# Mixture-of-experts stage in two multiplication passes of 32 places, with packed 2 MB weight loads and two more load places

## The chip, the core and the metric

One Trainium2 chip, of which this program uses one core. Times are device microseconds (us) of one launch, the median of 3 runs. The core has TensorE (PE) for matrix products, with weight loads (PEld) that overlap the products, VectorE (DVE), ScalarE (ACT), GpSimd (POOL) and SyncE (SP, which here only issues DMAs). Lines such as L323 are lines of the kernel before.

## The reference, cut to what matters

256 tokens of width 1024 go through two blocks in float32. The first has a mixer, a cross-attention and a mixture of experts; the second has feed-forward layers, sparse attention and a gated mixer. The change sits in the mixture of experts:

```python
D_MODEL = 1024; SEQ = 256; N_EXPERTS = 32; TOP_K = 2; D_EXPERT = 512
def hierarchical_moe(xn, w_rg, b_rg, w_re, b_re, w_g, w_u, w_d):
    ...                      # a group of 8 experts, then the best 2 of the group, for each token
    def expert_block(args):
        xb, e = args         # the tokens of one expert
        hb = jax.nn.silu(xb @ w_g[e]) * (xb @ w_u[e])
        return hb @ w_d[e]
    ...
    y = y_pad[dest] * gates[order][:, None]
    out = jnp.zeros((t, d), xt.dtype).at[token_idx[order]].add(y)
x = x + hierarchical_moe(rms_norm(x, norm_ffn[l]), ...)
```

`w_g` and `w_u` are 1024x512 and `w_d` is 512x1024 for each expert: 6.29 MB an expert in float32, 201.3 MB for all 32. 256 tokens by 2 experts make 512 assignments. In the reference's inputs (seed 0) the fullest expert gets 29 of them.

## The kernel before

Every large weight is streamed once. `weight_plan` lists the stages' weights as pieces of 128 partitions by up to 2048 columns (1 MB). `fetch` loads a piece into a `raw` place (R_RAW = 4 places of 1 MB; in the expert stage the two tiles `xh` and `xl` of the pool "moe" serve once as spare places) by a DMA on the SP queue, straight from the weight's own layout, so that a partition's row of a DMA is 512 to 4096 bytes long. `prepare` splits a piece into a high part `wh` (a cast on ACT, L296) and the rest `wl` (a subtraction on DVE, L297), both of type fp32r. Of `wh` and `wl` there are three places each (R_W = 3): `ahead` prepares the piece that lies two beyond the one in use, so a cast waits until PE is done with the piece three before it. A `raw` place is free once the subtraction has read it.

The activations are split in the same way, and `mm3` (L322 to L324) makes each product out of three passes: high by high, high by low, low by high.

In `moe`, the router on DVE computes which two experts each token takes, and its place among that expert's tokens. While that runs, ACT scales the tokens by the norm (L942, into `xs`), casts them to `xsh` (L943), and POOL makes `xsl` (L944), for one half of the tokens after the other. Each expert owns CAP = 42 places, three experts (EPB) fill a block of 128 places, and there are 11 blocks, two to a group. `prep` builds a 0/1 matrix `Sg` for a group, gathers tokens into places by products with it (L1056), with the norm's gain multiplied in when the result is split into `xh` and `xl` (L1060, L1061), and transposes `Sg` into `ST` (L1068, L1070). `expert_up` makes the gate and up products (2 weights x 8 rows x 3 passes = 48 products of 512 columns), the silu (L1229), the masked product `eh` (L1231), four transposes (L1234) and a split (`ehh` L327, `ehl` L328). `down` makes 4 x 2 x 3 = 24 products more, summed over the three experts of a block in PSUM. At a block's end `gathered` scales and splits the result into `yh` and `yl` (L1086, L1087), and `spread` adds it to the tokens by products with `ST` (L1096 to L1098). If an expert had more than 42 tokens, `overflow` would run all 32 experts again over all tokens, behind a branch on the loaded flag `rflag`.

The tile framework's scheduler sets the order of the instructions of each engine; it interleaves the code's pieces, as the rows in the section on the change show. An engine takes its instructions in that order. The stages follow one another as in `STAGES`: mix, cross, moe, fin1, f00, ma, f01, f10, mb, f11, fin2. The last seven are called the second block here.

## Time and profile before

| | us |
|---|---|
| median of 3 runs | 1921.79 (1920.49 to 1922.55) |
| the profiled execution | 1921.77 |
| its span on the core | 1920.0 |
| its expert stage, from the first expert's products to the second block's | 219.5 to 816.5, that is 597.0 |
| routing, between the last product of the cross-attention and the first of the experts | about 198 to 219.5 |

The profile gives, for each engine, how long it was busy and in how many instructions, what an instruction's engine waited for ahead of it, and what the DMAs moved. A product's busy time overlaps the next one's; the pace is the distance between two starts. Where DMA is given a share, it is the mean busy share of the core's 16 DMA engines.

### The profile page before, as it was taken

What the parts mean: (1) busy time and instruction counts of PE and PEld (TensorE: products, weight loads), DVE (VectorE), ACT (ScalarE), POOL (GpSimd) and SP (SyncE); (2) the same over time, 40 slices, a digit from 0 to 9 for tenths busy, and PEclk for the clock granted to TensorE, in tenths of its full rate; (3) what the DMA queues carried; (4) which work ended last, traced back from release to release, by engine and by line L of the source; (5) the groups of instructions that cost most, each with busy time, mean ns of one, the idle gap of its engine ahead of it and who ended that gap; (6) DMA issues with size and microseconds to landing.
All of it is one profiled execution on the core that took longest, in us unless ns stands there. A gap on an engine that the chain in (4) does not pass through costs nothing. (4 is left out here: it accounts for less than half of the span.)

```text
span 1920.0 us, 23872 instructions
## 1 busy us (share of the span) xinstructions
PE 1882.6 (98%) x9268; PEld 1572.8 (82%) x9268; DVE 1357.6 (71%) x1751; ACT 1071.3 (56%) x1318; POOL 30.6 (2%) x43
## 2 busy tenths in 40 slices
PE   8999699999999999999999999999999999999998
PEld 7888588878888888788889988888888888888886
DVE  6986888889888888875549755545554669566554
ACT  5755676777767777654444554444444544455443
POOL 1000100000000000000000000000000000000000
PEclk9999899999999999999999999999999999999999
DMA  8344499999999999966456455556555855666552
GB/s 269 117 169 153 147 335 332 335 330 334 344 329 346 334 342 337 334 208 211 171 181 199 160 163 188 177 175 203 189 178 177 294 178 176 185 199 194 177 185 77
DMA packets 264180, 438.39 MB, mean 228 GB/s; under 512 B 10784, under 2 KB 133936, under 8 KB 263680
## 3 DMA queue, kind: packets, MB, share of 16 engines
q1 hardware_dynamic: 261136, 424.85, 66.0%
q0 software_dynamic: 2496, 11.32, 1.8%
q8 instruction: 74, 1.21, 0.3%
q10 hardware_dynamic: 432, 0.66, 0.1%
q14 instruction: 42, 0.34, 0.1%
HBM read 435.67 MB, written 2.63 MB: 228 GB/s over the span
## 5 line engine op out<-in xcount | busy, mean ns | idle before, releaser
L297 DVE TENSOR_TENSOR wl<-raw,wh 128x2048 fp32r<-128x2048 f32 (+2 forms) x603 | 931.0, 1564 | 406.5 <-ACT wh L296 404.6
L296 ACT CAST wh<-raw 128x2048 fp32r<-128x2048 f32 (+2 forms) x603 | 780.4, 1322 | 498.4 <-PE acc L324 329.9
L322 PE MATMUL acc<-wh,xh 128*128 128x512 f32 x1424 | 561.6, 394 | 0.7 <-PEq L1167 0.7
L323 PE MATMUL acc<-wl,xh 128*128 128x512 f32 x1424 | 559.0, 393 | 3.1 <-DVE wl L297 2.1
L324 PE MATMUL acc<-wh,xl 128*128 128x512 f32 x1424 | 556.6, 391 | 0.0
L323 PEld LDWEIGHTS acc<-wl,xh 128*128 128x128 f32 x1424 | 267.6, 188 | 64.3 <-DVE wl L297 11.4
L322 PEld LDWEIGHTS acc<-wh,xh 128*128 128x128 f32 x1424 | 267.5, 188 | 54.6 <-ACTq L1167 0.8
L324 PEld LDWEIGHTS acc<-wh,xl 128*128 128x128 f32 x1424 | 267.4, 188 | 54.7
L322 PE MATMUL acc<-wh,hhi 128*128 128x512 f32 x352 | 137.6, 391 | 0.0
L324 PE MATMUL acc<-wh,hlo 128*128 128x512 f32 x352 | 137.0, 389 | 0.0
L323 PE MATMUL acc<-wl,hhi 128*128 128x512 f32 x352 | 137.0, 389 | 0.0
L322 PE MATMUL acc<-xh,wh 128*128 128x256 f32 x352 | 102.0, 291 | 2.3 <-ACT wh L290 2.3
L324 PE MATMUL pmi<-wh,ehl 128*128 128x512 f32 x256 | 101.5, 397 | 0.0
L324 PE MATMUL acc<-xh,wl 128*128 128x256 f32 x352 | 101.2, 289 | 0.3 <-DVE wl L291 0.3
L323 PE MATMUL acc<-xl,wh 128*128 128x256 f32 x352 | 101.4, 289 | 0.0
L323 PE MATMUL pmi<-wl,ehh 128*128 128x512 f32 x256 | 100.5, 393 | 0.0
L322 PE MATMUL pmi<-wh,ehh 128*128 128x512 f32 x256 | 94.9, 395 | 0.0
L601 ACT ACTIVATE sg<-acc,rs_o 128x256 f32<-128x256 f32 x66 | 31.3, 475 | 94.1 <-PE acc L324 94.0
L324 PEld LDWEIGHTS acc<-wh,hlo 128*128 128x128 f32 x352 | 66.1, 188 | 13.8
L323 PEld LDWEIGHTS acc<-wl,hhi 128*128 128x128 f32 x352 | 66.1, 188 | 13.6
L322 PEld LDWEIGHTS acc<-wh,hhi 128*128 128x128 f32 x352 | 66.1, 188 | 13.4
L322 PEld LDWEIGHTS acc<-xh,wh 128*128 128x128 f32 x352 | 67.9, 194 | 3.8 <-ACT wh L290 2.7
(409 smaller groups left out, 2043.5 us busy)
## 6 DMA issues: line engine op xcount, KB each, us to landing
raw<-in_ffn_w_in_dram SPq DMA_DIRECT2D x176, 512.0 KB, 4.8
raw<-in_w_e_gate_dram SPq DMA_DIRECT2D x64, 1024.0 KB, 7.0
raw<-in_w_e_down_dram SPq DMA_DIRECT2D x64, 1024.0 KB, 7.0
raw<-in_w_e_up_dram SPq DMA_DIRECT2D x62, 1024.0 KB, 7.1
raw<-in_ffn_w_out_dram SPq DMA_DIRECT2D x40, 1024.0 KB, 5.0
raw<-in_a_w_in_dram SPq DMA_DIRECT2D x14, 1024.0 KB, 5.1
raw<-in_b_w_in_dram SPq DMA_DIRECT2D x12, 1024.0 KB, 5.5
raw<-in_b_w_in_dram SPq DMA_DIRECT2D x16, 768.0 KB, 4.5
```

The source lines that it names most:

```text
L296: self.nc.scalar.copy(h[:, ks], raw[:, ks])
L297: self.nc.vector.tensor_tensor(l[:, ks], raw[:, ks], h[:, ks].bitcast(F32), ALU.subtract)
L322: mm(ps, ah, bh, start=start, stop=False)
L323: mm(ps, ah, bl, start=False, stop=False)
L324: mm(ps, al, bh, start=False, stop=stop)
L601: nc.scalar.activation(sg, ps[:, :256], AF.Silu, scale=rstd[:, t:t + 1])
```

## The change

**Two passes.** CAP is 32, EPB is 2, so a block of 128 places holds for each of two experts 32 places of high parts and beside them 32 of low parts of the same tokens. One operand `xb` so holds both parts, and each weight is multiplied in two passes, by `wh` and by `wl` (L1135, L1136, L1165, L1166 of the kernel after; 48 products of 512 columns an expert in place of 72). The four products high and low by high and low are then all there; high and low places are added by a product with a 0/1 matrix `fold` of 32 columns, which also transposes: 8 products of type float32 an expert (`act`, L1147), for which ACT first copies each PSUM result to `eg0` or `eg1` (L1138). The transposes, the mask and the split of 512 columns go; silu, product and split are now 128 columns wide (L1149 to L1153) and write into `eh0` or `eh1`, whose other half stays zero. There are 16 blocks in 8 groups of 4 experts. A gather writes 128 places for each part (L1093) and is cast by ACT alone (L1095). `y` is no longer split: `spread` multiplies `ST` and `y` in float32 (L1126), one half of tokens and columns at a time, taken from a list `todo`, one an expert.

**The norm's gain** is multiplied in ahead of the gather: POOL loads `norm_ffn` and multiplies the tokens by it into `xs` (L980), for each half of the tokens, with one `xs` for both.

**Loads.** The class `Plan` takes the place of `weight_plan`. The host lays every streamed weight out in the order of use, two pieces side by side, so that one DMA of 2 MB reads 16 KB in a row for each partition. (The first six pieces of the program are loaded one by one.) There are R_RAW = 2 places of 2 MB, free when the second piece has been prepared, and MORE = 2 places more for the loads of the stages cross and moe.

```diff
-R_RAW = 4
+R_RAW = 2
-CAP = 42
-EPB = 3
+CAP = 32
+EPB = 2
+NB = NE // EPB
+GE = 4
+MORE = 2
...
+        key, place, members = self.plan.loads[i]
+        pool = self.free.pop(0)
+        raw = pool.tile([P, 4096], F32, name=self.n("raw"), tag="raw")
+        width, at = sum(self.plan.cols(j) for j in members), 0
+        self.nc.sync.dma_start(raw[:, :width],
+                               self.io["w_" + key][place:place + P * width].rearrange("(p c) -> p c", p=P))
...
+        if self.plan.load_of.get(i + 1) != self.plan.load_of[i]:
+            self.free.append(pool)
...
+            if self.more is not None and self.plan.loads[self.fetched][0] not in ("cross", "moe"):
+                self.free = [pool for pool in self.free if pool is not self.more]
...
+                nc.gpsimd.tensor_tensor(xs, self.x[:, t], gb, ALU.mult)
+                nc.scalar.activation(xs, xs, AF.Copy, scale=rstd[:, t:t + 1])
...
+                    for part, src in enumerate((xsh, xsl)):
+                        for t in range(NT):
+                            nc.tensor.matmul(pt[:, part * P:(part + 1) * P], src[:, t, k * P:(k + 1) * P], Sg[:, t],
+                                             start=t == 0, stop=t == NT - 1)
+                    nc.scalar.copy(xb[:, k].rearrange("p (e a s) -> p e a s", a=2, s=CAP),
+                                   pt.rearrange("p (a e s) -> p e a s", a=2, s=CAP))
...
+                for n, (ST, y) in enumerate(blocks):
+                    nc.tensor.matmul(pu, ST[:, t * P:(t + 1) * P], y[:, hf], start=n == 0, stop=n == len(blocks) - 1)
...
+                        nc.tensor.matmul(ps, xb[:, kk], wh[:, k], start=kk == 0, stop=False)
+                        nc.tensor.matmul(ps, xb[:, kk], wl[:, k], start=False, stop=kk == KD - 1)
+                sb = self.t(pool, [P, 512], "eg" + str(w), 2)
+                nc.scalar.copy(sb, ps)
...
+                for w in range(2):
+                    for k in range(4):
+                        nc.tensor.matmul(ph[:, w, k], gu[w][:, k * P:(k + 1) * P], fold, start=True, stop=True)
+                sg = self.t(pool, [P, 4, CAP], "esg", 2)
+                nc.scalar.activation(sg, ph[:, 0], AF.Silu)
+                nc.vector.tensor_tensor(sg, ph[:, 1], sg, ALU.mult)
+                h, o = hs[e % EPB], (e % EPB) * 2 * CAP
+                nc.scalar.copy(h[:, :, o:o + CAP], sg)
+                nc.vector.tensor_tensor(h[:, :, o + CAP:o + 2 * CAP], sg, h[:, :, o:o + CAP].bitcast(F32), ALU.subtract)
...
+                    nc.tensor.matmul(yb[hf], h[:, kk], wh[:, kk % 2, cs], start=first and kk == 0, stop=False)
+                    nc.tensor.matmul(yb[hf], h[:, kk], wl[:, kk % 2, cs], start=False, stop=end and kk == 3)
```

Three places in the order of the instructions follow; a number behind a name is that of its buffer.

TensorE before, within one expert's down products (`pmi` is their PSUM tile, L322 to L324 the three passes, L1234 the transposes of the next expert):

```order
L324 MATMUL pmi_3145<-wh_3384,ehl_3294 128x512
L323 MATMUL pmi_3146<-wl_3385,ehh_3293 128x512
L324 MATMUL pmi_3146<-wh_3384,ehl_3294 128x512
L1234 MATMUL ptr_3422<-pack_77,eh_3420 128x128 x4
L322 MATMUL pmi_3145<-wh_3384,ehh_3293 128x512
L323 MATMUL pmi_3145<-wl_3385,ehh_3293 128x512
L324 MATMUL pmi_3145<-wh_3384,ehl_3294 128x512
```

After the transposes of the next expert, the passes over `ehh` and `ehl` go on three by three. TensorE after, from the end of one expert's down products into the next gate products (`acc`; L1093 is a gather, L1147 the fold, L1126 the spread):

```order
L1165 MATMUL pmi_3676<-wh_3662,eh_2113 128x512
L1166 MATMUL pmi_3676<-wl_3663,eh_2113 128x512
L1165 MATMUL pmi_3677<-wh_3662,eh_2113 128x512
L1166 MATMUL pmi_3677<-wl_3663,eh_2113 128x512
L1093 MATMUL ptr_3720<-Sg_3574,xsh_2117 128x128 x2
L1093 MATMUL ptr_3720<-Sg_3574,xsl_2118 128x128 x2
L1135 MATMUL acc_3726<-wh_3680,xb_3079 128x512
L1147 MATMUL ptr_3755<-pack_87,eg_3631 128x32 x4
L1147 MATMUL ptr_3755<-pack_87,eg_3674 128x32 x4
L1126 MATMUL ptr_3827<-y_3292,ST_2841 128x512
L1136 MATMUL acc_3726<-wl_3681,xb_3079 128x512
```

The product by `ehl` has gone, and eight folds and a float32 spread stand between two products of a gate.

ScalarE before, over two experts (L296 casts pieces, L1229 is the silu, L327 the split's cast):

```order
L1229 ACTIVATE esg_4001<-acc_3927 128x512
L296 CAST wh_3967<-raw_3884 128x2048
L296 CAST wh_3985<-raw_3928 128x2048
L327 CAST ehh_4010<-ptr_4005 128x512
L296 CAST wh_4020<-raw_3946 128x2048
L296 CAST wh_4038<-raw_3965 128x2048
L1060 ACTIVATE xh_3756<-ptr_4054,pack_77 128x256
```

A silu, then casts with single casts or scalings of other tiles between them. ScalarE after (L332 casts pieces, now two of one `raw` load in a row, L1138 copies a PSUM result, L1149 is the silu, L1152 the cast into `eh`, L1095 the gather's):

```order
L332 CAST wh_3903<-raw_3770 128x2048
L332 CAST wh_3915<-raw_3770 128x2048
L1138 COPY eg_3927<-acc_3900 128x512
L332 CAST wh_3933<-raw_3799 128x2048
L332 CAST wh_3945<-raw_3799 128x2048
L1149 ACTIVATE esg_4013<-ptr_4004 128x128
L332 CAST wh_3978<-raw_3858 128x2048
L332 CAST wh_3990<-raw_3858 128x2048
L1138 COPY eg_4002<-acc_3975 128x512
L1152 CAST eh_2114<-esg_4013 128x4x32
L1095 CAST xb_4091<-ptr_4092 128x256
```

After every second cast there is now a copy, silu or cast that waits for a product of PE.

GpSimd before, during routing:

```order
L927 DMA esel_2141<-in_c_esel_dram 128x352
L929 IOTA iota_2143 128x256
L262 DMA gb_7092<-in_norm_final_dram 128x1024
L944 TENSOR_TENSOR xsl_2151<-xs_2152,xsh_2150 128x1024
L944 TENSOR_TENSOR xsl_2151<-xs_2156,xsh_2150 128x1024
L1166 TENSOR_LOAD rflag_2221
```

The two subtractions follow each other with nothing of POOL's own between them. GpSimd after (L980 is the product with the gain, L983 the subtraction that was L944):

```order
L295 DMA gx_2119<-in_norm_ffn_dram 128x1024
L980 TENSOR_TENSOR gx_2119<-x,gx_2119 128x1024
L963 IOTA iota_2115 128x128
L971 MEMSET eh_2113 128x512
L971 MEMSET eh_2114 128x512
L983 TENSOR_TENSOR xsl_2118<-gx_2119,xsh_2117 128x1024
L980 TENSOR_TENSOR gx_2119<-x,gx_2119 128x1024
L983 TENSOR_TENSOR xsl_2118<-gx_2119,xsh_2117 128x1024
```

The second product with the gain stands between the two subtractions.

## Rows read from the trace of the kernel before

**Rows 1.** Four stretches, cut at the routing and at the ends of the expert stage: busy us of PE, PEld, DVE, ACT and POOL (instructions in brackets), granted TensorE clock, DMA share, GB/s.

```profile
0.00:200.00 200.00, 186.80 (x1158) 161.21 (x1158) 151.04 (x372) 123.22 (x264) 10.69 (x15) 1.00 0.56 181
200.00:219.50 19.50, 9.07 (x49) 8.41 (x49) 16.61 (x63) 7.96 (x16) 4.73 (x2) 0.65 0.21 83
219.50:816.50 597.00, 592.52 (x2739) 483.23 (x2739) 523.46 (x394) 429.09 (x347) 0.00 (x0) 1.00 0.95 330
816.50:1920.00 1103.50, 1094.24 (x5325) 920.00 (x5323) 666.48 (x923) 511.07 (x694) 15.16 (x26) 1.00 0.57 184
```

**Rows 2.** Waits within the expert stage (219.5 to 816.5): who waited for whom, us in total, times, longest.

```profile
DVE wl L297 <- ACT wh L296: 60.6, 95, 1.9
...
ACT wh L296 <- PE acc L324: 22.0, 35, 2.1
ACT wh L296 <- DMA raw<-in_w_e_down_dram: 21.3, 24, 2.2
```

**Rows 3.** PE's instructions in order of time (start us, us) at two places of the expert stage: products of 512 columns and gathers of 256; gathers of 128 columns, and four records of float32 products of 32 columns.

```profile
603.29 0.39 PE L322 MATMUL acc<-wh,xh 128*128 128x512 f32 x1
...
605.33 0.40 PE L322 MATMUL acc<-wh,xh 128*128 128x512 f32 x1
605.57 0.28 PE L1056 MATMUL ptr<-Sg,xsh 128*128 128x256 f32 x1
605.69 0.28 PE L1056 MATMUL ptr<-Sg,xsl 128*128 128x256 f32 x1
...
750.27 0.27 PE L1056 MATMUL ptr<-Sg,xsl 128*128 128x128 f32 x1
...
750.94 0.27 PE L1056 MATMUL ptr<-Sg,xsl 128*128 128x128 f32 x1
...
753.89 0.62 PE L1073 MATMUL ptr<-rG,Sg 128*128 128x32 f32 x4
```

**Rows 4.** Float32 products of 384 columns in the second block, as a group over the whole run (8 channel groups by 2 halves of the tokens are 16 products in the code).

```profile
L1464 PE MATMUL ptr<-vn,wsT 128*128 128x384 f32 x32 | 11.6, 485 | 0.0
```

**Rows 5.** The chain that ended last, at one place of the second block: the time at which PE had the chain, and the us of four records of the group in rows 4.

```profile
1617.30 1.29 PE ptr L1464 x4
```

**Rows 6.** Groups of instructions of one form within the expert stage: busy us, mean ns of one, and behind the bar the idle time ahead of them.

```profile
L297 DVE TENSOR_TENSOR wl<-raw,wh 128x2048 fp32r<-128x2048 f32 x184 | 419.6, 2289 | 58.6 <-ACT wh L296 57.9
L296 ACT CAST wh<-raw 128x2048 fp32r<-128x2048 f32 x184 | 349.9, 1906 | 62.2 <-DMA raw<-in_w_e_down_dram 21.3 <-PE acc L324 19.4 <-DMA raw<-in_w_e_up_dram 13.7
...
L1231 DVE SCALAR_TENSOR_TENSOR eh<-acc,pack,esg 128x512 f32<-128x512 f32 x32 | 24.0, 749 | 11.0 <-PE acc L324 11.0
L328 DVE TENSOR_TENSOR ehl<-ptr,ehh 128x512 fp32r<-128x512 f32 x32 | 21.9, 684 | 0.0
...
L1229 ACT ACTIVATE esg<-acc 128x512 f32<-128x512 f32 x32 | 19.1, 597 | 21.3 <-PE acc L324 21.0
L327 ACT CAST ehh<-ptr 128x512 fp32r<-128x512 f32 x32 | 18.8, 588 | 49.3 <-PE ptr L1234 49.3
L1087 DVE SCALAR_TENSOR_TENSOR yl<-pmi,gcol,yh 128x512 fp32r<-128x512 f32 x22 | 16.3, 745 | 0.0
...
L1086 ACT ACTIVATE yh<-pmi,gcol 128x512 fp32r<-128x512 f32 x22 | 15.2, 691 | 11.6 <-PE pmi L324 11.6
...
L1060 ACT ACTIVATE xh<-ptr,pack 128x256 fp32r<-128x256 f32 x32 | 14.7, 475 | 13.1 <-PE ptr L1056 13.1
L1061 DVE SCALAR_TENSOR_TENSOR xl<-ptr,pack,xh 128x256 fp32r<-128x256 f32 x32 | 14.3, 477 | 0.0
L1098 DVE TENSOR_TENSOR x<-ptr,x 128x512 f32<-128x512 f32 x22 | 14.1, 682 | 0.1
L297 DVE TENSOR_TENSOR wl<-raw,wh 128x512 fp32r<-128x512 f32 x18 | 11.4, 686 | 2.5 <-ACT wh L296 2.5
L296 ACT CAST wh<-raw 128x512 fp32r<-128x512 f32 x20 | 11.0, 617 | 2.6 <-PE acc L324 2.6
...
L1070 ACT CAST ST<-ptr 128x256 fp32r<-128x256 f32 x9 | 3.4, 372 | 6.4 <-PE ptr L1068 6.2
```

**Rows 7.** What the DMAs moved in the expert stage: packets, MB, mean rate, and the packets under three sizes.

```profile
DMA packets 85089, 196.92 MB, mean 330 GB/s; under 512 B 3059, under 2 KB 7485, under 8 KB 85053
```

**Rows 8.** Ten microseconds of the second block, and the stretch of the expert stage with the highest rate, with the columns of rows 1.

```profile
1525.00:1535.00 10.00, 10.00 (x46) 8.29 (x45) 9.48 (x13) 6.00 (x9) 1.08 (x2) 1.00 1.04 384
...
640.00:680.00 40.00, 40.00 (x188) 32.96 (x187) 33.69 (x25) 29.15 (x23) 0.00 (x0) 1.00 1.01 349
```

**Rows 9.** Loads of 1 MB in the second block between 1240 and 1290: count, KB each, median us from issue to landing.

```profile
raw<-in_ffn_w_out_dram SPq DMA_DIRECT2D x8, 1024.0 KB, 5.0
```

**Rows 10.** Routing in order of time (start us, us; in brackets the idle time ahead, and what ended it).

```profile
201.12 2.39 POOL L944 TENSOR_TENSOR xsl<-xs,xsh 128x1024 fp32r<-128x1024 f32 x1 [6.66 <-ACT xsh L943]
201.22 2.50 DVE L960 SCALAR_TENSOR_TENSOR r2eq<-rme,rm,pack 128x32 f32<-128x32 f32 x2
...
206.35 2.34 POOL L944 TENSOR_TENSOR xsl<-xs,xsh 128x1024 fp32r<-128x1024 f32 x1 [2.84 <-ACT xsh L943]
206.46 2.31 DVE L1026 TENSOR_TENSOR rG<-rG,rtm 128x64 f32<-128x64 f32 x1
...
210.44 0.55 PE L1056 MATMUL ptr<-Sg,xsh 128*128 128x256 f32 x1 [4.30 <-DVE rpp L1045]
...
215.91 0.28 PE L1056 MATMUL ptr<-Sg,xsl 128*128 128x256 f32 x1
```

More of the change, by code (lines that the diff above doesn't have):

```diff
@@ L198, in weight_plan, with mix @@
-    return plan, starts
+                self.add(kk, 512, (w[k0 * P:(k0 + kk) * P, half * 512:half * 512 + 512], 0, 512))
+    def mix(self):
+        w = self.w["w_in"][0]
+        for i in range(2):
+            self.add(KD, 256, (w[:, i * P:i * P + P], 0, P), (w[:, 256 + i * P:256 + i * P + P], P, P), pair=True)
+        self.b(w, 512, 1)
+        self.add(KD, P, (w[:, 2824 - P:2824], 0, P))
+        self.b(w, 768, 4)
+        self.a(w, (1792, 512))
+        self.a(w, (2304, 512))
+        self.b(self.w["w_ckv"][0], 0, 2)
+        self.o(self.w["w_out"][0], KD)
@@ new lines, in cross, with moe, down @@
+    def cross(self):
+        self.b(self.w["w_cq"][0], 0, 2)
+        self.a(self.w["w_ckv"][0], (512, 512))
+        self.o(self.w["w_co"][0], 4)
+    def moe(self):
+        def down(e):
+            for kp in range(2):
+                self.add(2, 1024, (self.w["w_e_down"][0, e][kp * 256:kp * 256 + 256], 0, 1024),
+                         place=None if kp else (e * 3 + 2) * P * 4096)
+        for e in range(NE):
+            self.a(self.w["w_e_gate"][0, e], (0, 512), place=e * 3 * P * 4096)
+            self.a(self.w["w_e_up"][0, e], (0, 512), place=(e * 3 + 1) * P * 4096)
+            if e:
+                down(e - 1)
+        down(NE - 1)
@@ new lines, in packed @@
+    def packed(self):
+        out = {"w_" + k: np.empty(n, np.float32) for k, n in self.size.items()}
+        for key, place, members in self.loads:
+            width, at = sum(self.cols(i) for i in members), 0
+            rows = out["w_" + key][place:place + P * width].reshape(P, width)
+            for i in members:
+                kk, n, parts, _ = self.pieces[i]
+                to = rows[:, at:at + kk * n].reshape(P, kk, n)
+                for src, off, cols in parts:
+                    to[:, :, off:off + cols] = src.reshape(kk, P, cols).transpose(1, 0, 2)
+                at += kk * n
+        return out
@@ L308, in ahead @@
     def ahead(self, i):
-        while self.prepared <= min(i + R_W - 1, len(self.plan) - 1):
+        while self.prepared <= min(i + R_W - 1, len(self.plan.pieces) - 1):
             self.fetch_more()
@@ L314, in fetch_more @@
     def fetch_more(self):
-        while self.fetched < len(self.plan) and (self.live < R_RAW or self.spare):
+        while self.fetched < len(self.plan.loads):
+            if self.more is not None and self.plan.loads[self.fetched][0] not in ("cross", "moe"):
+                self.free = [pool for pool in self.free if pool is not self.more]
+            if not self.free:
+                break
             self.fetch(self.fetched)
@@ L1104, in down @@
+            def down(e):
+                b, h = e // EPB, hs[e % EPB]
+                first, end = e % EPB == 0, e % EPB == EPB - 1
+                if first:
                     st["y"] = [self.pmi() for _ in range(2)]
-                    back.append((st["b", b][0],) + tuple(self.t(pool, [P, 2, 512], q, 2, F32R) for q in ("yh", "yl")))
                 yb = st["y"]
@@ L1129, in down @@
                         part(kk, hf, *w[kk // 2])
-                    gathered(b, hf, yb)
-                    spread(hf)
+                    gathered(hf)
+                    for t in range(NT):
+                        spread(back, hf, t)
                     if norm2 is not None:
@@ L1524, in body @@
                     net.moe(0 if following == "fin1" else None)
+                    more.close()
                 elif s == "f00":
@@ L1558 @@
     given = layout(given)
+    plan = Plan(given, STAGES)
+    given.update(plan.packed())
+    for n in STREAMED:
+        del given[n]
     arrays, io = {}, {}
@@ L1564 @@
     with tile.TileContext(nc) as tc:
-        body(tc, io, out)
+        body(tc, io, out, plan)
     r = _run(nc, [arrays], core_ids=[0])
```

407 lines of the change are left out of this document (178 added, 229 removed).

## The prediction

> **What bounds the kernel now.** I read the stretches first. The expert stage is 597.0 us of the 1920.0 us span, with PE busy 592.52, DVE 523.46, ACT 429.09 and the DMAs at a share of 0.95 and 330 GB/s [rows 1]. The reader should see two things: PE leaves 4.5 us free, and nothing else is far behind, so PE can be relieved only until it meets the loads or DVE. In the second block PE is busy 1094.24 of 1103.50 us, with the DMAs at 0.57; the first 200 us are at 0.56 [rows 1]. A better load can earn little there.
>
> Next the waits of the expert stage. ACT's casts of weights waited for PE 22.0 us in all and for one weight's loads 21.3, and DVE's subtraction for ACT 60.6 [rows 2]. Casts, subtractions and products are thus coupled through the three `wh` and `wl` places, but little time was lost by it: PE was never idle long.
>
> Third the paces of PE, as distances of starts. Ten products of 512 columns start between 603.29 and 605.57; nine steps from 603.29 to 605.33 make 0.227 us each. A gather of 256 columns takes 0.12 (605.57 to 605.69), one of 128 columns 0.11 (six steps from 750.27 to 750.94), a record of a float32 product of 32 columns 0.113, which is (0.62 - 0.28) / 3 [rows 3]. For wide float32 products only the second block has rows: 32 records for 16 products [rows 4], so two records a product, and four records of 384 columns in 1.29 us [rows 5]. That is 0.32 a record, 0.43 at 512 columns, 0.86 a product: nearly four times one pass.
>
> As a proof of the method, PE before: 72 x 32 = 2304 products x 0.227 = 523; 128 transposes x 0.11 = 14; gathers 128 x 0.12 + 16 x 0.11 = 17; 84 spread products x 0.227 = 19; about 50 small float32 records x 0.113 = 6. Sum 579, and the stage took 597, a factor of 1.03.
>
> **The change part by part: the expert stage.**
>
> PE: 48 x 32 = 1536 products x 0.227 = 349 (174 fewer). The fold is new: 256 products, two records each, x 0.113 = 58. The spread goes from 84 cheap products to 64 float32 ones x 0.86 = 55. Gathers: 7 groups x 32 x 0.11 = 25 (the first group is in routing). 28 transposes of `Sg` x 0.11 = 3, and 56 gate records x 0.113 = 6. Sum 496, or 15.5 an expert. Nearly half of what the third pass gives back is spent on float32 products.
>
> DVE [rows 6]: away go `eh` 24.0, `ehl` 21.9, `yl` 16.3, `xl` 14.3 and the additions to `x` 14.1, together 90.6. For 128 columns no row stands alone; from 0.686 at 512 and 2.289 at 2048 columns a step costs 0.53 per 512 columns and 0.15 whatever the width, so an estimate of 0.29. Added are 64 steps of it for silu's product and `eh` (19), 32 additions to `x` x 0.682 (22), 32 copies of `Sg` (9), and some 4 for more groups. 523.5 - 90.6 + 54 = 487. The weights' subtractions, 419.6 of it, stay.
>
> ACT [rows 6]: away go 19.1 + 18.8 + 15.2 + 14.7 = 67.8. Added are 64 copies of PSUM results x 0.588 (38), 64 steps of 128 columns (by the same reckoning from 0.617 and 1.906: 0.29) for silu and cast (19), 32 scalings into `y` x 0.691 (22), 56 casts of the gathers between 0.372 and 0.475 (24), 7 more `ST` x 0.372 (3). 429.1 - 67.8 + 106 = 467.
>
> DMAs: the bytes stay, 196.92 MB in the stage, now in rows of 16 KB; before, nearly all packets were under 8 KB [rows 7]. No row shows rows of 16 KB. From below in rate, the best stretch of the expert stage had 349 GB/s at a share of 1.01; from above, ten microseconds of the second block, with rows of 2 KB, had 384 at 1.04 [rows 8]. By 384 the stage needs 513 us, by 349 it needs 564. I take 384: the engines have done it with shorter rows, so 349 is not where they end. Could longer rows go beyond 384? No row says so; the floor below allows for it.
>
> So four resources stand at 513 (loads), 496 (PE), 487 (DVE) and 467 (ACT). Before, PE was far ahead of the others and the stage took 1.03 of its work. With four so close each will wait for the others more. The nearest row is the loads' own share of 0.95 [rows 1], the most they held over a whole stage; 1 / 0.95 = 1.05. 513 x 1.05 = 540, against 597: **-57**. The floor is PE alone, with loads at 400 GB/s or more: 496 x 1.03 = 511, that is -86.
>
> **Routing.** PE waits 4.30 us there for DVE's places, until 210.44; POOL's two subtractions take 2.39 and 2.34, and a DVE step of 32 or 64 columns that ran beside each took 2.50 and 2.31 [rows 10]: POOL's long steps also hold DVE up. The change adds two products on POOL, of the same 1024 columns, so 2.37 each as an estimate. The second stands between the two subtractions, and `xs` of the second half waits for the first half's `xsh` and `xsl`; behind it wait ACT's scaling and cast, POOL's second subtraction, and the gather that reads its result. POOL's idle 2.84 ahead of that subtraction [rows 10] would hold the product, but it was spent waiting for ACT, which now comes after. The first product needs no norm and may hide in the cross-attention. Bounds 0 and 4.7 (two products); I take one and a half, **+3.5**. The queue of SP is passed by nothing new but fewer, larger loads; POOL's queue gains one small load of the gain, long before.
>
> The first gather, from 210.44 to 215.91 and a little more [rows 10], ran partly at a lower clock (granted 0.65 over the stretch [rows 1]); it now writes half the columns in as many products. It gains up to half of its 5.5 us, unless ACT's eight casts at 0.42 take their 3.4 anyway: **-1** (-2.7 to 0).
>
> **Stage's end and the rest.** Before the last expert's down products stands copy 0.59, fold 16 x 0.113, silu, product, cast and subtraction 4 x 0.29, 3.6 us with little other work left; before, silu, `eh`, cast and split took 0.60 + 0.75 + 0.59 + 0.68 = 2.6 and four transposes. The last spreads are float32. **+2** (0 to 4).
>
> In the second block only the load places change. A piece's 24 products take 24 x 0.227 = 5.5 us and a load of 1 MB landed after 5.0 [rows 9]; two places of 2 MB hold as many bytes as four of 1 MB, but come free only when both halves have been prepared. It hides as long as a load of 2 MB, 5.5 us at 384 GB/s, lands within the 11 us that PE takes for two pieces. If that cover failed once at a stage's start, it would cost about 5; the 9.3 us that PE is idle there [rows 1] are all there is to gain. **0** (-9 to +5).
>
> Sum against the profiled 1921.77 (which is the median to 0.02, with 1.77 outside the span): -57 + 3.5 - 1 + 2 = -52.5, so **1869**. With the stage's factor between 1.01 and 1.08 it is 1848 to 1884.
>
> **The rivals.**
>
> *Floor: the loads cease to bind.* Were 16 KB rows good for 400 GB/s or more, PE would set the pace, 511 for the stage: 1921.8 - 86 + 4.5 = 1840, and 1831 with routing and gather at their low ends. For it: the 1.04 share at 384 came with short rows. Against: ACT and DVE are within 6% of PE and share its places.
>
> *R1: longer rows bring nothing.* The loads stay at the 349 GB/s of the expert stage's best stretch. Then they alone bind, 564 us, times 1.01 to 1.03: 570 to 581, and the time is 1899 to 1910. For it: at 0.95 and 330 GB/s the stage's full share is worth 347, just the 349 of its best stretch [rows 1, 8]. Against: 384.
> The Trainium skill ("DMA: Bandwidth & Descriptors", section "Where 436 GB/s comes from") puts HBM to SBUF transfers at about 358 GB/s a core, whatever the rows, since HBM binds. By that page the stage's loads would take 550 us as an estimate, and the time, with 1.03, would be 1896; its chance is counted with R1's. The 384 GB/s over ten microseconds [rows 8] speak against it as a ceiling; whether it holds over a whole stage no row shows.
>
> *R2: the three places couple the engines; this one ends slower.* With two passes a piece is used up in 8 x 0.227 = 1.82 us, and then its place must be cast (1.91) and subtracted (2.29): a round of 6.02 us. Six pieces in three places make two rounds an expert, 12.0 us. In a round nothing else may lie between; but the engines have other work: (496 - 349) / 32 = 4.6 on PE, 1.5 on DVE, 3.2 on ACT, 9.3 an expert. What of it falls into the rounds adds up instead of overlapping. Were half of it there, 16.7 an expert or 533, which the 540 covers; two thirds give 18.2, 582, 1911; all gives 21.3, 682 and about 2011. Slower than before begins at 18.5 an expert (592 plus the 4.5 outside), that is at 6.5 of the 9.3. For it: ACT after takes a copy, silu or cast that waits for PE between pairs of casts, and PE's eight folds and float32 spread stand between two products of a gate, as the order shows. Against: before, with the same three places, ACT's casts waited only 22.0 us for `acc` products [rows 2], and DVE could still be busy 523 of 597.
>
> *The added branch.* If an expert had over 32 tokens, `overflow` would run; 48 float32 products x 0.86 x 32 are 1321 us more, about 3190. With the reference's inputs the fullest has 29.
>
> **How the numbers follow.** Forecast, 1848 to 1890: 57%. Floor, below 1848: 14%, a third of it below 1838. R1, 1899 to 1910: 14%. R2 in part, 1890 to 1915: 7%. R2 whole, slower: 7%. The branch: 1%. The range of 1838 to 1911 leaves out 5 of the floor, 3 of R2 in part, 7 of R2 whole, and the branch, 16 in 100. About 0.2% (4 us) is what a measurement of this kernel can tell from no change. Within it fall 4% (R2 near its break-even); slower 7%; faster 89%.
>
> **What would show it.** Expert stage near 540 us; loads at 365 GB/s over it (197 / 540) and above 380 in its best stretches. If they stay at 349 or under with a share near 1, R1; if the share is well under 0.95 while PE, DVE and ACT each idle for another, R2. The 1536 products at 0.227, 512 fold records at 0.113, 128 spread records near 0.43; DVE near 487 and ACT near 467. Routing: PE's first gather some 3 us later; second block 1103.5 as before. I am wrong if the fold's small products cost more than 0.113 beside wide ones, or if the loads of the second block come late.

## The result, and the profile after

The kernel after takes 1869.01 us (median of 4 runs, 1868.4 to 1870.9) against 1921.99 of the kernel before beside it: a ratio of 0.9727, 95% interval 0.971 to 0.9744. The forecast was 1869. That agreement is an accident of two errors that cancel, and most of what follows is about them.

The four stretches, cut as in [rows 1], and behind them the middle of the expert stage:

```profile
0.00:198.70 198.70, 186.96 (x1158) 160.82 (x1158) 148.87 (x363) 122.05 (x262) 13.29 (x17) 1.00 0.51 195
198.70:223.70 25.00, 10.77 (x50) 10.49 (x49) 17.18 (x75) 8.30 (x16) 7.07 (x3) 0.52 0.00 1
223.70:749.10 525.40, 513.35 (x2482) 407.51 (x2482) 473.00 (x387) 444.97 (x444) 0.61 (x1) 0.99 0.94 373
749.10:1869.10 1120.00, 1104.51 (x5329) 926.38 (x5329) 665.52 (x920) 511.19 (x692) 15.14 (x26) 0.99 0.49 182
...
280.00:700.00 420.00, 417.39 (x2040) 332.29 (x2040) 386.88 (x311) 359.38 (x346) 0.61 (x1) 1.00 0.98 391
```

Routing begins here where the last product ahead of the router ends, at 198.2 before and 198.7 after. That product transposes the router's own logits (L937 before, L978 after); the table of times before calls it the last of the cross-attention, but that one ended at 192.2 and 192.6. Cut at the same events (this product, the first product of the experts, the first of the second block), the kernel before has 198.2, 21.4, 596.9 and 1103.5 us, the kernel after 198.7, 25.0, 525.4 and 1120.0. So the expert stage gained 71.5 us, 14.5 more than the 57 of the forecast, and the second block, forecast at no change, gave 16.5 back. In the middle of the stage PE is busy 417.39 of 420 us and the DMAs are at a share of 0.98 and 391 GB/s; which of the two holds the stage is the first question of the experiments. Over the whole stage DVE was busy 473.00 us and ACT 444.97, 14 and 22 under the forecast's 487 and 467.

Waits in the expert stage, as in [rows 2]:

```profile
DVE wl L333 <- ACT wh L332: 40.3, 47, 3.2
ACT wh L332 <- PE acc L1135: 19.1, 21, 2.1
...
ACT eg L1138 <- PE acc L1136: 10.1, 14, 1.7
...
ACT wh L332 <- DMA raw<-in_w_f_dram: 1.7, 1, 1.7
...
PE acc L1136 <- DVE wl L333: 1.3, 6, 0.4
```

The one wait for a load that is left is the second block's first ([rows 2] had 21.3 us on the down loads alone): no cast waited for a load of expert weights. DVE's wait for ACT fell from 60.6 to 40.3. The groups that answer to [rows 6], and the new ones on PE, with the bytes as in [rows 7]:

```profile
L333 DVE TENSOR_TENSOR wl<-raw,wh 128x2048 fp32r<-128x2048 f32 x186 | 418.7, 2288 | 36.3 <-ACT wh L332 35.1
L332 ACT CAST wh<-raw 128x2048 fp32r<-128x2048 f32 x186 | 349.2, 1910 | 30.5 <-PE acc L1135 17.0 <-PE pmi L1165 13.5
...
L1147 PE MATMUL ptr<-pack,eg 128*128 128x32 f32 x512 | 63.4, 267 | 3.0 <-ACT eg L1138 2.6 <-ACT ST L1109 0.4
L1126 PE MATMUL ptr<-y,ST 128*128 128x512 f32 x120 | 62.4, 612 | 2.1 <-DVE esg L1150 2.1
...
L1138 ACT COPY eg<-acc 128x512 f32<-128x512 f32 x64 | 37.7, 588 | 13.6 <-PE acc L1136 10.1
...
L1149 ACT ACTIVATE esg<-ptr 128x128 f32<-128x128 f32 x32 | 8.8, 276 | 17.5 <-PE ptr L1147 17.5
```

```profile
DMA packets 13569, 196.01 MB, mean 373 GB/s; under 512 B 1504, under 2 KB 1504, under 8 KB 1632
```

The 512 fold records and the spread are there; steps of 128 columns take 0.276 (estimate: 0.29). 85089 packets became 13569.

Where the second block lost 16.5 us, by the same events in both traces: up to the sparse attention's first score +2.5 (the last eight spread records run there now, where four passes did before), from there to the first product that weighs `av` +7.4, from there to the gated mixer's first transpose of `ws` +2.1 (a stretch of 441 us, with two feed-forward layers in it), from there to the first product with `yTh` +4.7, the rest -0.1. Below, these are the attention's part, the stretch up to `ws` and the one behind it. In the sparse attention, PE's wait, and the granted clock from there on (columns as in [rows 1]):

```profile
959.95 3.92 PE L1347 MATMUL pmi<-aki,aqi 64*128 64x128 f32 x16 [1.70 <-DMA aki<-aki]
```

```profile
957.00:960.00 3.00, 1.30 (x11) 1.02 (x9) 2.60 (x6) 2.24 (x4) 0.00 (x0) 1.00 0.13 48
960.00:966.00 6.00, 6.00 (x26) 4.70 (x26) 4.10 (x13) 2.30 (x4) 0.00 (x0) 0.58 0.33 98
966.00:975.00 9.00, 9.00 (x32) 6.88 (x32) 4.91 (x21) 1.57 (x3) 0.00 (x0) 0.52 0.40 168
```

`aki` is one half of the partitions copied onto the other by a small DMA. It now lands so late that PE stands still for 1.70 us, and then PE runs near the lower of its levels, 1.2 GHz (granted 0.58 and 0.52), for some 15 us. The chain that ended last shows the transfers by name (start, us), here of the kernel after:

```profile
953.93 5.97 DMA aki<-aki
...
1452.38 20.79 DMA bb<-in_b_b_in_dram
...
1479.44 8.94 DMA raw<-in_w_mb_dram
```

and of the kernel before, where the chain went through `aki` too, but not through `bb`:

```profile
1018.80 4.36 DMA aki<-aki
```

`bb` is a row of 512 biases copied to all partitions. The view of its tile gives its DMAs' times from issue to landing, before:

```profile
DMA to landing us min/median/max: 3.4/3.9/14.5
```

and after:

```profile
DMA to landing us min/median/max: 3.6/5.6/20.8
```

The longest is the first in both. At the gated mixer's start `bb` stands on GpSimd's queue behind `lng` and `lnb` (1.5 MB each) and `ws`, while SP asks for four loads of 2 MB. The new stalls of PE are these two, with what ended them, and behind them two waits of the same place:

```profile
1474.17 0.47 PE L362 MATMUL acc<-wh,xh 128*128 128x512 f32 x1 [1.82 <-DVE zz L1452]
...
1491.95 0.22 PE L1447 MATMUL ptr<-pack,bs 8*128 8x8 f32 x1 [3.04 <-ACT wsT L1445]
```

```profile
DVE zz L1452 <- DMA bb<-in_b_b_in_dram: 8.6, 1, 8.6
ACT wh L332 <- DMA raw<-in_w_mb_dram: 5.3, 1, 5.3
```

The second stall is a weight load that comes late. While DVE waits 8.6 us for `bb`, it frees no load place, so the load of `w_mb` at 1479.44 is asked for late and lands 8.94 us later. ACT's next cast waits 5.3 us for it, and the copy `wsT` that PE needs stands behind that cast.

Routing, as in [rows 10]:

```profile
191.72 2.37 POOL L980 TENSOR_TENSOR gx<-x,gx 128x1024 f32<-128x1024 f32 x1 [33.43 <-DVE x L569]
...
201.68 2.39 POOL L983 TENSOR_TENSOR xsl<-gx,xsh 128x1024 fp32r<-128x1024 f32 x1 [6.47 <-ACT xsh L982]
...
204.15 2.34 POOL L980 TENSOR_TENSOR gx<-x,gx 128x1024 f32<-128x1024 f32 x1
...
204.33 2.17 DVE L1058 TENSOR_TENSOR rex<-rm 128x2 f32<-128x2 f32 x1
...
212.82 0.45 PE L1093 MATMUL ptr<-Sg,xsh 128*128 128x128 f32 x1 [4.14 <-DVE rpp L1083]
...
214.99 0.41 PE L1093 MATMUL ptr<-Sg,xsh 128*128 128x128 f32 x1
215.20 0.63 PE L1093 MATMUL ptr<-Sg,xsl 128*128 128x128 f32 x2
215.63 0.41 PE L1093 MATMUL pmi<-Sg,xsh 128*128 128x128 f32 x1
```

GpSimd's first product with the gain runs ahead of routing, at 191.72, the second between the subtractions; a DVE step on 2 columns takes 2.17 us beside it (0.15 before, at 203.77). From the start of routing the first gather starts 14.1 us later (12.3 before), and from there the first expert 10.9 later (9.1 before). The gathers of 128 columns start 0.21 us apart, at a granted 0.52 over the stretch. Before, the granted clock was full again for the last part of routing; after, it was not (first line before, second after):

```profile
216.00:219.60 3.60, 2.72 (x21) 2.17 (x19) 2.39 (x10) 2.17 (x6) 0.00 (x0) 1.00 0.00 0
...
216.00:220.00 4.00, 4.00 (x21) 4.00 (x21) 0.00 (x0) 1.81 (x6) 0.00 (x0) 0.50 0.00 0
```

### The profile page after: what moved, and what is told of

Its sections match the earlier page's. It is cut to its first block, busy times and chain, and to the rows that moved or that the text cites. A ratio compares the mean times of both kernels' runs of the same rounds, so it can differ in the third digit from the quotient of the medians.

```text
span 1869.1 us, 22766 instructions
## 1 busy us (share of the span) xinstructions
PE 1815.6 (97%) x9018; PEld 1505.2 (81%) x9018; DVE 1304.6 (70%) x1743; ACT 1086.5 (58%) x1413; POOL 36.1 (2%) x47
## 5 line engine op out<-in xcount | busy, mean ns | idle before, releaser
L333 DVE TENSOR_TENSOR wl<-raw,wh 128x512 fp32r<-128x512 f32 (+3 forms) x605 | 929.5, 1566 | 392.0 <-ACT wh L332 389.8
L332 ACT CAST wh<-raw 128x512 fp32r<-128x512 f32 (+3 forms) x605 | 779.2, 1325 | 458.2 <-PE acc L364 332.6
L362 PE MATMUL acc<-wh,xh 128*128 128x512 f32 x912 | 362.6, 398 | 2.6 <-DVE zz L1452 1.8
L363 PE MATMUL acc<-wl,xh 128*128 128x512 f32 x912 | 357.8, 392 | 0.0
L364 PE MATMUL acc<-wh,xl 128*128 128x512 f32 x912 | 357.1, 392 | 0.0
L1135 PE MATMUL acc<-wh,xb 128*128 128x512 f32 x512 | 212.4, 415 | 3.6 <-ACT wh L332 3.0
L1136 PE MATMUL acc<-wl,xb 128*128 128x512 f32 x512 | 213.4, 417 | 1.3 <-DVE wl L333 1.3
L1135 PEld LDWEIGHTS acc<-wh,xb 128*128 128x128 f32 x512 | 97.1, 190 | 30.2 <-issue 9.6
L1136 PEld LDWEIGHTS acc<-wl,xb 128*128 128x128 f32 x512 | 96.9, 189 | 28.8 <-issue 6.2
L1165 PE MATMUL pmi<-wh,eh 128*128 128x512 f32 x256 | 99.9, 423 | 0.0
L1166 PE MATMUL pmi<-wl,eh 128*128 128x512 f32 x256 | 98.6, 417 | 0.6
```

The costliest lines, as they stand in the source:

```text
L332: self.nc.scalar.copy(h[:, ks], raw[:, ks])
L333: self.nc.vector.tensor_tensor(l[:, ks], raw[:, ks], h[:, ks].bitcast(F32), ALU.subtract)
L362: mm(ps, ah, bh, start=start, stop=False)
L363: mm(ps, ah, bl, start=False, stop=False)
L364: mm(ps, al, bh, start=False, stop=stop)
L1135: nc.tensor.matmul(ps, xb[:, kk], wh[:, k], start=kk == 0, stop=False)
```

## The experiments

Times are medians beside fresh runs of the kernel before (1921.1 to 1922.4 us); stage lengths are cut at the events named above.

**1. Are the loads or TensorE the limit of the stage?** Two runs take work from one of them.

```diff
+        half = key == "moe" and place // (P * 4096) % 3 == 2
-        self.nc.sync.dma_start(raw[:, :width],
+        self.nc.sync.dma_start(raw[:, :2048 if half else width],
...
+            if half:
+                at = 0
```

> The kernel after, but a down load reads only its first MB, and both of its pieces are prepared from that: a sixth of the expert bytes is left out, nothing else. Theory A (TensorE binds in the expert stage, the loads merely keep up at a share of 0.94): stage 522 to 528 us, the time 1865 to 1872. Rival B (the loads bind, at 391 GB/s and a share of 0.98 in the middle of the stage): the stage falls to TensorE's 500 to 511, the time 1844 to 1856.

```diff
-                    ST = self.t(pool, [P, S], "ST", 5)
+                    ST = self.t(pool, [P, S], "ST", 5, F32R)
...
-                    back.append((st["b", b][0], self.t(pool, [P, 2, 512], "y" + str(b % 2), 2)))
+                    back.append((st["b", b][0], self.t(pool, [P, 2, 512], "y" + str(b % 2), 2, F32R)))
```

> The kernel after, but y and ST are of type fp32r, so a spread product is one pass of 0.23 us instead of 0.86; the low part of y is left out. It takes 40 us of work from TensorE and nothing from the loads. Theory A (TensorE binds): the stage falls by 22 to 38 us until the loads bind near 400 GB/s (491 us), the time is 1833 to 1848. Rival B (the loads bind): stage within 5 us of 525, the time 1864 or more.

Measured: half_down 1875.63, ratio 0.9752 (0.9737 to 0.9767), stage 531.0; spread_1pass 1866.37, ratio 0.9701 (0.9683 to 0.9718), stage 525.0. In the first run theory B fails (the stage is even 3 us past A's range), in the second theory A: neither relief shortens the stage. For the loads the trace says why. By the landing times, each load of expert weights in the kernel after landed at least 1.8 us (median 5.3) before the first cast of a whole piece that reads it, and at least 1.6 us in spread_1pass; nothing waited for them, whatever their share. What PE was spared went into other waits. In spread_1pass:

```profile
ACT eg L1138 <- PE acc L1136: 21.5, 38, 1.1
...
PE acc L1136 <- DVE wl L333: 13.5, 14, 1.8
```

In the kernel after these were 10.1 and 1.3. (ACT's order differs a little in spread_1pass.) So PE and the coupling of PE, ACT and DVE through the `wh` and `wl` places stand at about the same length, and the loads are not the limit. So both at once (the two edits together):

> The kernel after with both reliefs at once: a down load reads only its first MB (a sixth of the expert bytes is left out), and a spread product is one pass (the low part of y is left out). Theory A (loads and TensorE are two equal limits near 525 us, so that either relief alone shows nothing): the stage falls by 30 to 42 us to where VectorE's 473 and TensorE's remainder stand, 483 to 495; the time is 1828 to 1842. Rival C (the three wh and wl places couple cast, subtraction and product, whatever work is taken away): the stage stays above 515, the time above 1857.

Measured: 1845.52, ratio 0.9595 (0.9579 to 0.9611), stage 506.0. Both theories miss: the stage is 11 to 23 us above the 483 to 495 that A reckoned, and 9 below C's 515. The middle of that stage:

```profile
280.00:680.00 400.00, 386.88 (x1965) 317.82 (x1963) 376.80 (x306) 351.20 (x344) 0.61 (x1) 1.00 0.89 337
```

PE is busy 97%, DVE 94%, ACT 88%: no one is free, and no one is full. Why the two edits together take 19 us is not shown. No cast of a whole piece waited for a load here either (the closest landed 2.0 us ahead), but the order is another. In the kernel after, 3 of the 64 copies `eg` stand between the two casts of one load; in both_less it is 14, in half_down 17. Those copies found PE done (no idle time ahead of them), but many other steps of ACT and PE moved too, and what that is worth was not measured.

**2. What do packed rows give?** First without the second pass saved: the kernel before with packed loads.

> The kernel before with the packed loads of the kernel after and nothing else: three passes, 42 places, two load places of 2 MB throughout (the moe pool leaves no room for the two more). Theory A (before, TensorE bound the expert stage at 579 x 1.03 and loads were no limit; the second block pays for packed loads): expert stage 588 to 600, second block 1112 to 1122, the time 1925 to 1940, slower than before. Rival B (the loads' 0.95 share held the stage up): expert stage 575 or less, the time 1915 or less.

Measured: 2066.18, ratio 1.0751 (1.0733 to 1.0769), expert stage 727.2, second block 1109.7. Slower, as A said, but far past A's range and by another mechanism:

```profile
ACT wh L337 <- DMA raw<-in_w_moe_dram: 193.3, 73, 4.8
DVE wl L338 <- ACT wh L337: 116.3, 74, 4.5
```

With two places of 2 MB, one is held until both of its pieces are prepared, so loads stop and go (275 GB/s at a share of 0.73). Two such places alone are too few for this kernel. The same with places as before:

```diff
-        if self.open and place is None and i >= FINE:
+        if self.open and place is None and i >= FINE and False:
...
-        raw = pool.tile([P, 4096], F32, name=self.n("raw"), tag="raw")
+        raw = pool.tile([P, 2048], F32, name=self.n("raw"), tag="raw")
```

> The kernel before (three passes, 42 places) with packed rows, but one piece of 1 MB a load (8 KB rows) and the four 1 MB places of before, without its two spare ones at the start of the expert stage. Theory A (TensorE bound the stage before, longer rows alone have nothing to shorten; packed_alone lost its time to having two places only): expert stage 585 to 600 us, the second block 1103 to 1110, the time 1908 to 1926. Rival B (rows, not TensorE, held the stage before): expert stage 575 or less, the time below 1900. Rival C (packed rows as such starve three passes): stage above 620.

Measured: 1922.87, ratio 1.0004 (0.9994 to 1.0013), expert stage 595.4, second block 1104.7. Theory A: with three passes, long rows have nothing to shorten, as PE's 592.52 of 597 in [rows 1] said.

Then the kernel after without the packed rows:

```diff
+            if True:
+                r = raw[:, at:at + kk * n].rearrange("p (k n) -> p k n", k=kk)
+                for src, off, cols in parts:
+                    self.nc.sync.dma_start(r[:, :, off:off + cols], src.rearrange("(k p) n -> p k n", p=P))
```

> The kernel after, its load places and the order of its loads kept, but each 1 MB piece of a load is read from the weight's own layout, in rows of 1 to 4 KB instead of one row of 16 KB for each partition. Theory A (packing gave the expert stage its 373 GB/s, and packing also delays the small transfers of the second block): loads fall back to at most the 349 GB/s that the kernel before reached, the expert stage goes from 525 to 564 to 581 us, the second block from 1120 back to about 1104; the time is 1890 to 1910. Rival B (row length doesn't matter; the two passes made room for the loads): expert stage 525, second block 1120, 1865 to 1873 in all.

Measured: 1953.46, ratio 1.0159 (1.0144 to 1.0175), expert stage 619.4, second block 1111.3. Slower than before, and slower than theory A's slow end. Packed loads of 1 MB (the edit of packed_1mb in the kernel after, with twice as many places) do nearly the same:

> The kernel after with one piece of 1 MB a load (8 KB rows), four places of 1 MB and four more in the first block, so the same bytes in places. Theory A (8 KB rows are long enough, and smaller loads hold up the small transfers of the second block less): expert stage 520 to 530 us, second block 1104 to 1114, the time 1853 to 1864. Rival B (the 16 KB rows and 2 MB loads are what gives 391 GB/s): expert stage 540 or more, the time 1875 or more.

Measured: 1945.27, ratio 1.0115 (1.0098 to 1.0131), expert stage 611.8, second block 1107.4. Theory B by its number. But the loads are not what is waited for. Waits of own_rows in its expert stage:

```profile
DVE wl L338 <- ACT wh L337: 126.1, 84, 3.8
ACT eg L1143 <- PE acc L1141: 117.5, 58, 3.8
PEld acc L1141 <- DVE wl L338: 59.8, 74, 2.1
PE acc L1141 <- DVE wl L338: 40.6, 51, 1.8
```

This is a ring: ACT waits for PE (to copy `eg`), DVE for ACT, PE for DVE; and no DMA in it. ACT's order shows why. In the kernel after (L332 casts, L1138 copies; start us, us, in brackets the idle time ahead):

```profile
481.26 3.75 ACT L332 CAST wh<-raw 128x2048 fp32r<-128x2048 f32 x2 [0.45 <-PE pmi L1165]
485.14 0.59 ACT L1138 COPY eg<-acc 128x512 f32<-128x512 f32 x1
```

In own_rows (the same lines are L337 and L1143):

```profile
486.30 3.71 ACT L337 CAST wh<-raw 128x2048 fp32r<-128x2048 f32 x2
492.83 0.59 ACT L1143 COPY eg<-acc 128x512 f32<-128x512 f32 x1 [2.83 <-PE acc L1141]
493.31 1.90 ACT L337 CAST wh<-raw 128x2048 fp32r<-128x2048 f32 x1
```

The scheduler put the copy, which waits for the last product of a gate, between the two casts of a load. The second cast, which PE needs next, stands behind it. Counted over the stage, 52 of the 64 copies stand so in own_rows and 51 in loads_1mb, against 3 in the kernel after, and those 52 waited 112.5 of the 117.5 us.

So the rate theory was in doubt, and the last run tells order from rows: own_rows with the instructions of ACT and PE tied, through the expert stage, to the order that they have in the kernel after.

```diff
+        for engine, count, order in ORDER:
+            of = [i for i in nc.cur_bb.bb.instructions if i.engine == engine and type(i).__name__ not in SKIP][-count:]
...
+            for a, b in zip(order, order[1:]):
+                tc.add_manual_dep(b, a.name, mybir.DependencyInfo(mybir.DependencyClass.NoSync, mybir.DependencyReason.DATA))
```

> The run own_rows again (each piece read from the weight's own layout, in rows of 1 to 4 KB, same load places), but through the expert stage ScalarE and TensorE take their instructions in exactly the order that they have in the kernel after; in own_rows the scheduler had put a copy of a PSUM result (eg) between the two casts of a load. Theory O (the order, not the rows, made own_rows' stage 619 us): stage 523 to 535 if own rows can carry 373 GB/s, the time 1858 to 1870. Theory O and R together (order and rows): the loads bind at 349 GB/s, stage 560 to 582, the time 1893 to 1917. Theory R (the rows alone): stage 608 to 625, the time 1940 or more.

Measured: 1874.62, ratio 0.9755 (0.9739 to 0.9771), expert stage 538.5, second block 1110.3. Of the 94 us between own_rows and the kernel after, the order is 81 and the rows are at most 13 (DVE's order, left to the scheduler, differs too). Its waits and the middle of its stage:

```profile
DVE wl L338 <- ACT wh L337: 37.9, 39, 2.5
ACT eg L1143 <- PE acc L1141: 22.9, 28, 1.7
```

```profile
280.00:700.00 420.00, 406.40 (x1981) 323.22 (x1981) 373.52 (x302) 349.73 (x336) 0.61 (x1) 0.99 1.01 376
```

The ring's wait fell from 117.5 to 22.9 us. The loads in short rows now run at 376 GB/s at a share of 1.01, 4% under the 391 of long rows. Whether they bind is not shown: no cast of a whole piece waited for one (the closest landed 1.4 us ahead), so the last 13 us stay open. That the order made most of the difference (theory O) is shown; the result is a little above its range. (ACT and PE were tied together, so which of the two orders matters more stays open.)

**3. The second block.** Does it pay for long rows? Own rows from there on (the edit of own_rows under the condition that the stage isn't mix, cross or moe):

> The kernel after, but from the second block on each piece is read from the weight's own layout, in rows of 1 to 4 KB; the first block's loads stay packed. Theory A (rows of 16 KB hold up the small transfers at the start of the gated mixer, two loads issued together those of the sparse attention): the second block takes 1110 to 1113 us as in the run with own rows throughout, the time is 1857 to 1863. Rival B (it was shorter there because its stages met another state of the load queue): 1866 or more.

Measured: 1868.78 (1860.77 to 1870.29), ratio 0.9712 (0.9685 to 0.974); second block 1113.9. In it the two stretches around `ws` are as before (441.0 and 53.8 us), the attention's part is not (85.3), and the expert stage of the profiled run was 3 us longer. So A in the mixer and not in the attention; the time itself is B's, and doesn't tell. The landing times fit: the longest of `bb` is 14.6 us here, 20.8 with 16 KB rows and 21.3 with 8 KB rows (loads_1mb), so it seems to go with the rows; `aki` takes 6.0 here, 5.97 in the kernel after and 3.7 in loads_1mb, so it seems to go with the 2 MB that are asked for at once. So the small transfers themselves:

```diff
-                nc.gpsimd.dma_start(ki[64:P], ki[0:64])
+                pk = self.ptr()[:, :S]
+                nc.tensor.matmul(pk, self.twice, ki[0:64], start=True, stop=True)
+                nc.scalar.copy(ki[64:P], pk[64:P])
...
+            for c in range(2):
+                self.bcast(bbs[c], io["b_b_in_2"][0, H + c * 512:H + (c + 1) * 512])
             self.bcast(lng, io["b_ln_g_2"][0])
```

> The kernel after, with two edits in the second block: in the gated mixer the first two bias rows bb are requested ahead of lng, lnb and ws; in the sparse attention the copy of aki onto the other 64 partitions is made by one TensorE product and a ScalarE copy instead of a DMA. Theory A (the 16.5 us that the second block lost are these two small transfers, late behind 2 MB loads, and the low clock after the first): the second block goes from 1120 to 1104 to 1109 us, the time is 1853 to 1858. Rival B (the loads of 2 MB themselves are late there, or the two places come free too late): within 5 us of the kernel after, 1864 to 1872.

Measured: 1864.29, ratio 0.97 (0.9684 to 0.9716), second block 1113.4. The attention's part is 77.4 us (85.0 after, 77.6 before) and the stretch up to `ws` 441.0: both as theory A says. But the one behind it went from 58.4 to 60.9, and the time is in B's range, since now `ws` is waited for in place of `bb`:

```profile
DVE ws L1449 <- DMA ws<-in_b_w_sp_dram: 7.7, 1, 7.7
```

With `ws` and `bs` also ahead of `lng` and `lnb`, and the gain moved from GpSimd:

```diff
-                nc.gpsimd.tensor_tensor(xs, self.x[:, t], gb, ALU.mult)
-                nc.scalar.activation(xs, xs, AF.Copy, scale=rstd[:, t:t + 1])
+                nc.vector.scalar_tensor_tensor(xs, self.x[:, t], rstd[:, t:t + 1], gb, op0=ALU.mult, op1=ALU.mult)
```

> The kernel after with three edits: in the gated mixer the first two bias rows, then ws and bs, are requested ahead of lng and lnb; aki is copied by TensorE and ScalarE; the norm's gain and factor are multiplied in by one VectorE instruction for each half of the tokens, in place of a GpSimd product and a ScalarE scaling. Theory A: second block 1120 to 1103 to 1107 us (the sparse attention's 7.6 us as in small_first, both waits of the mixer gone), routing 25.0 to 22 to 24, the time 1850 to 1857. Rival B (with the small rows first, ws or a load of w_mb is late in their place, and VectorE's gain delays the router as much as GpSimd's did): second block 1110 or more, routing 25, the time 1861 or more.

Measured: 1857.26, ratio 0.9658 (0.9645 to 0.9672): faster than both kernels. The second block takes 1106.1, its first four stretches 208.4, 77.4, 441.0 and 53.7: all of the loss is back but the spreads. (A cast still waits 4.0 us for a load of `w_mb`, but the stretch behind `ws` is as short as before, so there it costs PE nothing.) Routing is 25.3: theory A for the second block, B for the gain.

**4. Routing.** The other try on it:

```diff
+            xss = [xs, self.t(pool, [P, 2, 512], "y0", 2).rearrange("p a b -> p (a b)")]
             for t in range(NT):
-                nc.gpsimd.tensor_tensor(xs, self.x[:, t], gb, ALU.mult)
+                nc.gpsimd.tensor_tensor(xss[t], self.x[:, t], gb, ALU.mult)
```

> The kernel after, but the second half's tokens times the gain go to a buffer of their own (a y0 buffer that is idle then), so GpSimd makes both products ahead of its two subtractions. Theory A (the second product between the subtractions holds a VectorE step for 2.2 us and delays the second half's scaling, cast and subtraction): the first gather starts 2 to 5 us earlier than 212.8, the time is 1864 to 1867. Rival B (the first gather waits for the router's own steps on VectorE, which the product delays wherever it stands): within 1 us of the kernel after, 1868 to 1870.

Measured: 1870.27, ratio 0.9731 (0.9718 to 0.9744). The first gather starts at 213.1, no earlier: B, a little past its range. Routing as cut here is 23.0 us, 2.0 shorter, but it begins 2.3 us later, at 201.0, since a DVE step of the norm takes 2.22 us beside the second product and PE's products for the router's logits wait for what stands behind that step. The cost moves with the product. Made on DVE (best_small), two steps of 1.28 us are in the router's own chain. From the cross-attention's own last product the first gather starts 20.2 us later in the kernel after, 20.7 in gain_early, 20.3 in best_small, and 18.2 before: about 2 us for the gain in all three places.

## Why the time was right and its terms were not

**The expert stage, forecast -57, measured -71.5.** The products, folds and steps of 128 columns came near what was counted. The step that failed is the choice of the longest resource: "I take 384". It made the loads, at 513 us, the term that the stage is worked out from. They ran at 391 GB/s over 420 us, at which all of them need 196.9 / 391 = 504, and no cast waited for one: they ran as fast as their places came free. PE's 496 was the sum that mattered, and the stage took 1.06 of it. The factor of 1.05 was a fair size, the term under it was not; that the stage came within 15 us of the forecast is in part luck. That PE would not stand far ahead of the others any more was right: sparing it 40 us (spread_1pass) brought nothing, because the ring through the `wh` and `wl` places was as long.

**R1 (349 GB/s is the end)** is refuted for either row length: even own rows ran at 376 once the order let them. The bound was read from a stage in which PE set the pace, and the share of 1.01 over 40 us [rows 8] misled me: a share near 1 there didn't mean that no more bytes could go through.
The Trainium skill ("DMA: Bandwidth & Descriptors", "Where 436 GB/s comes from") gives about 358 GB/s a core for HBM to SBUF. Beside its measured table just ahead of that section, the Trainium skill says that this is about what each core gets with both cores of an HBM domain streaming. This program uses one core, and had 373 over 525 us and 391 over 420; so the 1896 was reckoned from a figure for another case.

**R2 (the three places couple the engines)** I held unlikely, and for the order that was built it didn't make the stage slower. But it is the mechanism with the largest lever here. With the copy of `eg` between two casts the stage is 612 to 619 us, 15 to 22 longer than before the change. I asked whether such a copy waits, and answered from the waits of the kernel before, where ACT's order is another. The prediction did read that the new copies stand between pairs of casts, but counted that for R2; that the pairs stay whole is what decided against it.

**Packed loads** I credited with rate. Their rows are worth at most 13 us of the stage with the order fixed, nothing with three passes (packed_1mb), and their 2 MB places without two more cost 130 us there (packed_alone). What one load of two pieces also did is change the order that the scheduler chose, worth 81.

**The second block, forecast 0 (-9 to +5), measured +16.5.** The step that failed: I asked only whether a load lands in time for its own pieces. I didn't ask what else uses the DMAs there. `aki`, `bb` and `ws` are small, PE's next products hang on them, and they now come later behind the loads: `aki` 4.36 to 5.97 us, `bb` 14.5 to 20.8, `ws` 14.1 to 21.5. One load did come late, as the prediction's last line feared: ACT waited 5.3 us for it, with a copy that PE needs behind that cast. 2.5 of the 16.5 are the spreads, forecast as +2 at the stage's end.

**Routing, forecast +3.5 and -1 for the gather, measured +1.8 and +1.8.** GpSimd's products hold DVE as forecast (2.17 us on 2 columns), but the first of the two ran ahead of routing, so one counts and not one and a half. The gather gains nothing from half the columns: at the lower level of the clock (1.2 GHz, granted 0.50) a gather started 0.21 us after the one ahead with 128 columns as with 256, and all of it ran there, while before the last gathers ran at the full clock, 0.12 apart.

**Sums and readings that were off,** none of which moves the forecast: the floor with routing and gather at their low ends comes to 1835, not 1831; the stage before had 32 gathers of 128 columns, not 16, which makes its sum 581; and the 2.50 us in [rows 10] are two DVE steps, not one.

## What to carry to other kernels

When a change brings several engines within a few per cent of each other, read the order of each engine for an instruction that waits on one neighbour and stands ahead of what another needs: here one copy between two casts was worth more than the choice of row length, and an innocent change of a load's shape can move it. When loads are made larger, look for the small transfers that share the DMAs with them, and for what PE does while it waits. A share near 1 doesn't name the limit: look whether an instruction waited, here for a load. And take the stages apart even when the total agrees.

## What was unexpected in the hardware

- A stop of 1.70 us of PE was followed by some 15 us at a granted 0.52 to 0.58 and cost 7.4 us in all.
- The DMAs carried 391 GB/s at a share of 0.98 in rows of 16 KB and 376 at 1.01 in rows of 2 to 4 KB, where the kernel before had 349 at 1.01 [rows 8]: the share alone doesn't give the rate that is left.
